# Root of the feed-forward norm: from columns on GpSimd to a row on VectorE, and four PSUM banks more for the first blocks

## The chip, the cores and the metric

The kernel runs on one core of a Trainium2 chip. The metric is device time in microseconds (us), from one launch to its end; lower is better. Five engines work beside each other: TensorE (PE in the profile, with its weight loads as PEld), VectorE (DVE), ScalarE (ACT), GpSimd (POOL) and SyncE (SP), which issues the transfers.

## The reference

One inference step of a two-layer decoder trunk runs over 256 prompt tokens and 8 x 8 sample tokens, 320 in all, with 1024 features. Layer 0 mixes tokens by a gated spatial MLP, layer 1 by an mLSTM. After either comes a feed-forward layer, and ahead of each of the four a norm. What the change touches is the norm ahead of the feed-forward layer and its first blocks:

```python
def rmsnorm(x, g):
    x32 = x.astype(jnp.float32)
    y = x32 * lax.rsqrt(jnp.mean(x32 * x32, axis=-1, keepdims=True) + EPS)
    return (y * g.astype(jnp.float32)).astype(x.dtype)

def conv_ffn(x, buf, w_up, conv_w, conv_b, w_down):
    up = x @ w_up
    a, g = jnp.split(up, 2, axis=-1)
    a_c, new_buf = causal_dwconv(a, buf, conv_w, conv_b)
    y = (jax.nn.gelu(a_c) * g) @ w_down
    return y, new_buf
...
        h = rmsnorm(x, norm_ffn_g[i])
        y, fb = conv_ffn(h, ffn_buf[i], f_w_up[i], f_conv_w[i], f_conv_b[i], f_w_down[i])
        x = x + y
```

All data is fp32.

## The kernel before

Activations stand features by tokens: `xT` is 8 blocks of 128 features by 320 tokens. A product with a weight matrix is made in blocks of 128 output features. `block` (L196) takes one PSUM bank `pm`, and for each of the 8 blocks of input features issues three matmuls of 320 columns (`rows`, L189). They are three because every fp32 operand is split into two fp32r halves, a high one and a low one (`xh`, `xl`, `wh`, `wl`), and high x high, high x low and low x high are summed. So a block of the up projection is 24 matmuls.

The norm's gain is folded into `xh` and `xl` when a residual is finished (`residual_norm`, L309), and the sums of squares are gathered there in `acc`, features on partitions, tokens along the row. The factor of each token, one over the root, is not known when the projection starts. It is applied when a block's result is read out of PSUM: `conv` and `gate` multiply by `rb`, a tile with the factor of all 320 tokens on every partition. So the first blocks of the projection can run before `rb` exists, but their banks stay taken until then.

`rb` is made in three steps. `norm_cols` (L242) makes six matmuls of two columns (three groups of tokens, each as two passes of fp32) that turn `acc` into columns with tokens on partitions (`pc`), VectorE adds the mean's factor and EPS (`ms`), and GpSimd raises the three columns to the power of -1/2 (`rc`). `norm_row` (L270) splits `rc` into halves, VectorE lays them on the diagonal (`dg`, four instructions), two matmuls with ones spread the diagonal to a row on all partitions (`pb`), and ScalarE copies that to `rb`.

In `ffn` (L356) the blocks come in groups of four: two of the conv branch, two of the gate branch. I call the blocks of the up projection p0, p1, p2 and so on. In the first group the order on PE was p0, `norm_cols`, p1, `norm_row`, p2, p3.

Weights come in pieces of 128 x 1024. SP loads them into `raw` (4 buffers), ScalarE casts the high half to `wh` (L167) and VectorE makes the low half `wl` (L168), 3 buffers each. PE's order is pinned to the order in the code; the other engines' queues are set by a scheduler, and each runs its own queue in order.

There are eight PSUM banks: three in the pool `psm`, from which `block` takes, and five in `psa`, for everything else.

Of the kernel before, what the change touches and what calls it, by code (L numbers as in the profile page):

```python
# [9 lines left out]

F32 = mybir.dt.float32
F32R = mybir.dt.float32r
AF = mybir.ActivationFunctionType
ALU = mybir.AluOpType
MULT, ADD, SUB, MAX = ALU.mult, ALU.add, ALU.subtract, ALU.max

P = 128
EPS = 1e-6
# [3 lines left out]
T = TP + NB * NS  # L22
D = 1024
KD = D // P
# [14 lines left out]
class Net:  # L39
# [23 lines left out]
    def weights(self):  # L63
# [19 lines left out]
        def ffn(l):  # L83
# [8 lines left out]
            if l:  # L92
                add(I["f_dnl"], 0, 4, 4, 4, k0=k0)

        ffn(0)
        add(I["b_wg"], 0, 8)
        for h in range(NH):
# [33 lines left out]
    def prefetch(self, n, m):  # L131
# [15 lines left out]
        while len(self.halved) < min(m, len(self.wq)):  # L147
# [6 lines left out]
            else:  # L154
                wh = self.wsp.tile([P, 8, P], F32R, tag="wh", name="wh")
                wl = self.wsp.tile([P, 8, P], F32R, tag="wl", name="wl")
            if self.wq[i][0] is self.I["b_wg"]:
# [35 lines left out]
            self.mm(ps[:, :T], wh[:, k, :], xl, False, False)  # L193
            self.mm(ps[:, :T], wl[:, k, :], xh, False, last and k == kn - 1)

    def block(self, kt, rhs):  # L196

        ps = self.psm.tile([P, 512], F32, tag="pm", name="pm")
        done = 0
        while done < kt:  # L200
            kn = self.wq[self.used][3]
            self.chunk(ps, lambda k: rhs(done + k), done == 0, done + kn == kt)
            done += kn
        return ps
# [5 lines left out]
    def norm_block(self, m, gcol):  # L210
# [3 lines left out]
        g = self.vec(gcol + m)  # L214
        nc.scalar.activation(self.xh[:, m, :], x, AF.Copy, scale=g)
        nc.vector.scalar_tensor_tensor(self.xl[:, m, :], x, g, self.xh[:, m, :].bitcast(F32), op0=MULT, op1=SUB)

    def square_block(self, m):
        nc = self.nc
        x = self.xT[:, m, :]  # L220
        if m == 0:
            self.acc = self.tp.tile([P, T], F32, tag="acc", name="acc", bufs=2)
            nc.scalar.activation(self.acc, x, AF.Square)
        else:
            self.sq = self.tp.tile([P, T], F32, tag="sq", name="sq", bufs=2)
            nc.scalar.activation(self.sq, x, AF.Square)
            nc.vector.tensor_tensor(self.acc, self.acc, self.sq, op=ADD)
# [42 lines left out]
    def norm_row(self):  # L270

        nc = self.nc
        rc = self.tp.tile([P, 2, 3], F32R, tag="rc2h", name="rc_hl", bufs=1)
        self.split(rc[:, 0, :], rc[:, 1, :], self.rc)
        dg = self.tp.tile([P, 2, T], F32R, tag="dg", name="dg", bufs=1)
        rc = rc.bitcast(F32)
        for half in range(2):
            nc.vector.tensor_tensor(
                dg[:, half, :TP].rearrange("p (t c) -> p t c", c=P), self.ident.unsqueeze(1).to_broadcast([P, 2, P]),
                rc[:, half, :2].unsqueeze(2).to_broadcast([P, 2, P]), op=MULT)  # L280
            nc.vector.tensor_scalar(dg[:, half, TP:], self.ident[:, 64:], rc[:, half, 2:3], None, op0=MULT)
        pb = self.psa.tile([P, 512], F32, tag="pa", name="pb")
        for half in range(2):
            self.mm(pb[:, :T], self.ones.bitcast(F32R), dg[:, half, :], half == 0, half == 1)
        rb = self.tp.tile([P, T], F32, tag="rb", name="rb", bufs=1)
        nc.scalar.copy(rb, pb[:, :T])
        self.rb = rb

    def bring(self, m):

        nc, I = self.nc, self.I
        if m == 0:
            nc.sync.dma_start(self.xv[:, :16 + T], I["x0"])
        else:
            nc.sync.dma_start(self.xT[:, m, :], I["xr"][m - 1])
# [31 lines left out]
    def layer_a(self):  # L327
        nc, tc, I, O = self.nc, self.tc, self.I, self.O
        with tc.tile_pool(name="ya", bufs=1) as yp, tc.tile_pool(name="la", bufs=1) as lp:
            yh = yp.tile([P, KA, T], F32R, name="yh_a")  # L330
            yl = yp.tile([P, KA, T], F32R, name="yl_a")
# [65 lines left out]
            def v_gelu(q, pv):  # L397
# [5 lines left out]
                for t in range(2):  # L403
                    nc.scalar.activation(v[:, t, cs], pv[t], AF.Gelu_apprx_tanh, scale=self.rc[:, t:t + 1])
                    nc.vector.bn_stats(st[:, t, q, :], v[:, t, cs])
                nc.scalar.activation(v[r, 2, cs], vs, AF.Gelu_apprx_tanh, scale=self.rc[r, 2:3])
                nc.vector.bn_stats(st[r, 2, q, :], v[r, 2, cs])
# [41 lines left out]
            def normalise(q):  # L449
                for t in range(3):  # L450
                    r = slice(64 if t == 2 else 0, P)
                    vv = v[r, t, q * 512:(q + 1) * 512]
                    nc.scalar.activation(vv, vv, AF.Identity, scale=rs[r, t:t + 1], bias=ve[r, t:t + 1])

# [56 lines left out]
    def ffn(self, l, gnext):  # L511
        nc, tc, I, O = self.nc, self.tc, self.I, self.O
        NPAD = 2 + TP + 10 * NB
        NC = NPAD - 2
        with tc.tile_pool(name=f"yf{l}", bufs=1) as yp, tc.tile_pool(name=f"lf{l}", bufs=1) as lp:
            ext = 0 if gnext is not None else 64
            yh = yp.tile([P, KF, T + ext], F32R, name=f"yh_f{l}")
            yl = yp.tile([P, KF, T], F32R, name=f"yl_f{l}")
            stt = lp.tile([P, KF, 16], F32, name=f"fst{l}")
            nst = lp.tile([P, KF, 18], F32, name=f"fns{l}")  # L520
            nc.sync.dma_start(stt, I["f_state"][l])
            pads = []
            for i in range(3):
                pd = lp.tile([P, NPAD], F32, name=f"fpad{l}_{i}")
                nc.gpsimd.memset(pd[:, 0:2], 0.0)
                pads.append(pd)
            gls = {}

            def conv(b, ps):
                pd = pads[b % 3]  # L530
                ps_ = pd[:, 258:].rearrange("p (b e) -> p b e", e=10)
                nc.gpsimd.tensor_copy(ps_[:, :, 0:2], stt[:, b, :].rearrange("p (b e) -> p b e", e=2))
                nc.vector.tensor_tensor(pd[:, 2:258], ps[:, :TP], self.rb[:, :TP], op=MULT)
                nc.vector.tensor_tensor(ps_[:, :, 2:10], ps[:, TP:T].rearrange("p (b e) -> p b e", e=8),
                                        self.rb[:, TP:].rearrange("p (b e) -> p b e", e=8), op=MULT)
                nc.gpsimd.tensor_copy(nst[:, b, 0:16].rearrange("p (b e) -> p b e", e=2), ps_[:, :, 8:10])
                nc.gpsimd.tensor_copy(nst[:, b, 16:18], pd[:, 256:258])
                cv = lp.tile([P, NC], F32, tag="cv", name="fcv", bufs=3)
                w = V_FW + 66 * l + b
                nc.scalar.activation(cv, pd[:, 0:NC], AF.Identity, scale=self.vec(w), bias=self.vec(V_FB + KF * l + b))  # L540
                for i in (1, 2):
                    nc.vector.scalar_tensor_tensor(cv, pd[:, i:i + NC], self.vec(w + i * KF), cv, op0=MULT, op1=ADD)  # L542
                gl = lp.tile([P, T], F32, tag="gl", name="fgl", bufs=4)
                nc.scalar.activation(gl[:, :TP], cv[:, :TP], AF.Gelu_apprx_tanh)
                nc.scalar.activation(gl[:, TP:].rearrange("p (b e) -> p b e", e=8),
                                     cv[:, 256:].rearrange("p (b e) -> p b e", e=10)[:, :, 2:10], AF.Gelu_apprx_tanh)
                gls[b] = gl

            def gate(b, ps):
                gl = gls.pop(b)  # L550
                y = self.tp.tile([P, T], F32, tag="yf", name="y_f", bufs=2)
                nc.vector.tensor_tensor(y, ps[:, :T], self.rb, op=MULT)
                nc.vector.tensor_tensor(y, y, gl, op=MULT)
                self.split(yh[:, b, :T], yl[:, b, :], y)
                if ext:
                    nc.gpsimd.tensor_copy(yh[:, b, T:], yl[:, b, TP:])

            for i in range(KF // 2):
                b = 2 * i
                p0 = self.block(KD, self.x_rhs)  # L560
                if i == 0:
                    self.norm_cols()
                    p1 = self.block(KD, self.x_rhs)
                    self.norm_row()
                    conv(b, p0)
                    conv(b + 1, p1)
                else:
                    conv(b, p0)
                    conv(b + 1, self.block(KD, self.x_rhs))
                gate(b, self.block(KD, self.x_rhs))  # L570
                gate(b + 1, self.block(KD, self.x_rhs))
            nc.sync.dma_start(O["f_state"][l], nst)
            rhs = lambda k: (yh[:, k, :T], yl[:, k, :])
            if gnext is not None:
                for m in range(KD):
                    self.residual_norm(m, self.block(KF, rhs), gnext)
            else:
                self.final(lambda m: self.block(KF, rhs), yh, yl, lp)
# [792 lines left out]
```

## Time and profile before

| | |
|---|---|
| median of 3 runs | 949.35 us (949.16 to 949.36) |
| the profiled execution | 949.44 us |
| its span, first to last instruction | 947.7 us |
| granted TensorE clock, mean | 0.999 |
| PE busy | 940.8 us (99%) |
| VectorE busy | 675.1 us (71%) |
| ScalarE busy | 517.7 us (55%) |
| GpSimd busy | 85.1 us (9%) |

Layer 0's feed-forward starts at 189.5 us of the span, layer 1's at 704.0 us. In the timeline a row has the start in us, the duration in us, the engine, the line, the operation and the tiles, out of what it reads; a bracket at its end is the idle time ahead of it and what ended that. Matmuls overlap: a row of 0.31 us is followed by the next one's start 0.147 us later, so the cost of a matmul in a stream is the distance of starts, not its duration.

### The profile page before, as it was taken

Reading aid. Unit: us, or ns where it says so; the run is one execution under the profiler, and the core shown is the slowest. Engines: PE = TensorE matmul, PEld = TensorE weight load, DVE = VectorE, ACT = ScalarE, POOL = GpSimd, SP = SyncE. Lnnn points to the kernel's source line nnn. Section 1 sums busy time; section 2 is a strip of 40 time slices with the busy share of each in tenths; the row PEclk is TensorE's granted clock in tenths of the full one; section 3 lists DMA queues with packets and bytes.
Section 4 is the critical chain, followed back from the end, with each engine's and each line's share of the span. In section 5 each row is a group of like instructions: output and inputs, shape, how many; then the busy total and the mean of one; then the engine's idle time right before and its main releaser. Section 6 shows DMA issues by size and latency. Waiting matters only on the chain.

```text
span 947.7 us, 17236 instructions
## 1 busy us (share of the span) xinstructions
PE 940.8 (99%) x6549; PEld 919.5 (97%) x6549; DVE 675.1 (71%) x1244; ACT 517.7 (55%) x940; POOL 85.1 (9%) x300
## 2 busy tenths in 40 slices
PE   9999999999999999999999999999999999999997
PEld 8789999999999999999999999999999999999997
DVE  6668985577777764458898987787778777775542
ACT  7557444354554444347787776575756455444332
POOL 2100000010000000003211001010011111100001
PEclk9999999999999999999999999999999999999999
DMA  8736344444444445456667555734474444445621
GB/s 288 222 126 180 128 141 144 148 153 143 149 156 151 144 148 157 147 169 224 227 204 230 191 187 198 250 124 145 161 213 145 145 157 155 139 147 153 200 85 57
DMA packets 58311, 156.97 MB, mean 166 GB/s; under 512 B 6916, under 2 KB 19852, under 8 KB 58228
## 3 DMA queue, kind: packets, MB, share of 16 engines
q1 hardware_dynamic: 58084, 155.61, 51.2%
q8 instruction: 52, 0.85, 0.4%
q14 instruction: 31, 0.25, 0.1%
q10 hardware_dynamic: 144, 0.26, 0.1%
HBM read 143.89 MB, written 11.95 MB: 164 GB/s over the span
## 4 chain that ended last, share of the span: by engine, by line
PE 99%; ACT 0%; POOLq 0%; DVE 0%; issue 0%; DVEq 0%; ACTq 0%
PE pm L48 83%; PE pv L48 5%; PE num L48 2%; PE pvs L48 2%; PE pyt L48 1%; PE pmix L48 1%; PE py L48 1%; PE psc L48 1%; PE pCp L48 1%; PE pcs L48 1%; PE pv L51 1%; PE phn L51 0%; PE pw L48 0%; PE pk L51 0%; PE pg L48 0%; PE pc L48 0%
## 5 line engine op out<-in xcount | busy, mean ns | idle before, releaser
L167 ACT CAST wh<-raw 128x1024 fp32r<-128x1024 f32 (+4 forms) x252 | 254.5, 1012 | 287.1 <-PE pm L48 154.2
L168 DVE TENSOR_TENSOR wl<-raw,wh 128x1024 fp32r<-128x1024 f32 (+4 forms) x252 | 296.0, 1178 | 117.2 <-ACT wh L167 114.4
L48 PE MATMUL pm<-xh,wh 128*128 128x320 f32 x1216 | 377.9, 311 | 0.0
L48 PE MATMUL pm<-xh,wl 128*128 128x320 f32 x1216 | 375.8, 309 | 0.0
L48 PE MATMUL pm<-xl,wh 128*128 128x320 f32 x1216 | 375.7, 309 | 0.0
L48 PEld LDWEIGHTS pm<-xh,wh 128*128 128x128 f32 x1216 | 228.3, 188 | 0.7
L48 PEld LDWEIGHTS pm<-xl,wh 128*128 128x128 f32 x1216 | 228.4, 188 | 0.0
L48 PEld LDWEIGHTS pm<-xh,wl 128*128 128x128 f32 x1216 | 228.3, 188 | 0.0
L48 PE MATMUL pm<-yh_f,wh 128*128 128x320 f32 x308 | 95.3, 309 | 0.0
L48 PE MATMUL pm<-yh_f,wl 128*128 128x320 f32 x308 | 95.0, 308 | 0.0
L48 PE MATMUL pm<-yl_f,wh 128*128 128x320 f32 x308 | 95.0, 308 | 0.0
L48 PEld LDWEIGHTS pm<-yl_f,wh 128*128 128x128 f32 x308 | 57.8, 188 | 0.0
L48 PEld LDWEIGHTS pm<-yh_f,wh 128*128 128x128 f32 x308 | 57.8, 188 | 0.0
L48 PEld LDWEIGHTS pm<-yh_f,wl 128*128 128x128 f32 x308 | 57.8, 188 | 0.0
L542 DVE SCALAR_TENSOR_TENSOR fcv<-fpad,vecs,fcv 128x336 f32<-128x336 f32 x88 | 49.5, 565 | 2.0 <-ACT fcv L540 0.6
L307 DVE TENSOR_TENSOR xT<-pm,xT 128x320 f32<-128x320 f32 x38 | 18.5, 490 | 31.4 <-PE pm L48 31.4
L48 PE MATMUL pm<-yhb,wh 128*128 128x320 f32 x128 | 40.3, 315 | 0.0
L48 PE MATMUL pm<-yh_a,wh 128*128 128x320 f32 x128 | 39.6, 309 | 0.0
L48 PE MATMUL pm<-yl_a,wh 128*128 128x320 f32 x128 | 39.5, 309 | 0.0
L48 PE MATMUL pm<-yh_a,wl 128*128 128x320 f32 x128 | 39.5, 309 | 0.0
L48 PE MATMUL pm<-yhb,wl 128*128 128x320 f32 x128 | 39.5, 309 | 0.0
L48 PE MATMUL pm<-ylb,wh 128*128 128x320 f32 x128 | 39.5, 309 | 0.0
(321 smaller groups left out, 1350.9 us busy)
## 6 DMA issues: line engine op xcount, KB each, us to landing
raw<-in_f_up SPq DMA_DIRECT2D x88, 512.0 KB, 3.5
raw<-in_b_win SPq DMA_DIRECT2D x48, 512.0 KB, 4.4
raw<-in_f_dn SPq DMA_DIRECT2D x28, 448.0 KB, 3.3
C<-in_C SPq DMA_DIRECT2D x32, 258.0 KB, 5.0
raw<-in_a_win SPq DMA_DIRECT2D x16, 512.0 KB, 3.5
raw<-in_a_wo SPq DMA_DIRECT2D x16, 512.0 KB, 3.6
out_Cs<-C SPq DMA_DIRECT2D x32, 256.0 KB, 3.8
raw<-in_f_dn SPq DMA_DIRECT2D x14, 512.0 KB, 3.5
```

Source lines behind the costliest of these rows:

```text
L48: self.pin(self.nc.tensor.matmul(out, lhsT, rhs, start=start, stop=stop))
L51: self.pin(self.nc.tensor.transpose(out, in_, ident))
L167: self.last_split = nc.scalar.copy(wh[:, c, :], raw[:, c, :])
L168: self.last_low = nc.vector.tensor_tensor(wl[:, c, :], raw[:, c, :], wh[:, c, :].bitcast(F32), op=SUB)
L307: self.nc.vector.tensor_tensor(x, ps[:, :T], x, op=ADD)
L542: nc.vector.scalar_tensor_tensor(cv, pd[:, i:i + NC], self.vec(w + i * KF), cv, op0=MULT, op1=ADD)
```

## The change

Both feed-forward layers lose `norm_cols` and `norm_row`; the two mixers keep them. In their place:

- `norm_spread` splits `acc` itself into two halves, `acc_h` on ScalarE and `acc_l` on VectorE.
- `norm_root` multiplies ones by these halves in two matmuls of 320 columns. The result `pb` holds every token's sum of squares on all partitions. VectorE then takes the root of the whole row: it makes `half` (minus half of the mean with EPS), a first guess from the bits as an integer, and three Newton steps of three instructions, and leaves the result in `rb`. These are 11 instructions on 128 x 320.
- The two matmuls stand inside p1, behind its first two of eight input blocks.
- The blocks p3 to p6 take their banks from `psa` and not from `psm`.

```diff
+I32 = mybir.dt.int32
...
-    def block(self, kt, rhs):
+    def block(self, kt, rhs, ps=None):
 
-        ps = self.psm.tile([P, 512], F32, tag="pm", name="pm")
+        if ps is None:
+            ps = self.psm.tile([P, 512], F32, tag="pm", name="pm")
...
+    def norm_spread(self):
+
+        nc = self.nc
+        ah = self.tp.tile([P, T], F32R, tag="yf", name="acc_h", bufs=2)
+        al = self.tp.tile([P, T], F32R, tag="yf", name="acc_l", bufs=2)
+        self.split(ah, al, self.acc)
+        return ah, al
+
+    def norm_root(self, ah, al):
+
+        nc = self.nc
+        pb = self.psa.tile([P, 512], F32, tag="pa", name="pb")
+        for i, a in enumerate((ah, al)):
+            self.mm(pb[:, :T], self.ones.bitcast(F32R), a, i == 0, i == 1)
+        half = self.tp.tile([P, T], F32, tag="acc", name="half", bufs=2)
+        y = self.tp.tile([P, T], F32, tag="rb", name="rb", bufs=1)
+        s = self.tp.tile([P, T], F32, tag="sq", name="root", bufs=2)
+        nc.vector.tensor_scalar(half, pb[:, :T], -0.5 / D, -0.5 * EPS, op0=MULT, op1=ADD)
+        nc.vector.tensor_scalar(y.bitcast(I32), half.bitcast(I32), -0.5, float(0x5f3759df - 2 ** 30 - 2 ** 22), op0=MULT, op1=ADD)
+        for _ in range(3):
+            nc.vector.tensor_tensor(s, y, half, op=MULT)
+            nc.vector.tensor_tensor(s, s, y, op=MULT)
+            nc.vector.scalar_tensor_tensor(y, s, 1.5, y, op0=ADD, op1=MULT)
+        self.rb = y
...
+            def blk(i, j):
+                return self.block(KD, self.x_rhs, self.psa.tile([P, 512], F32, tag="pa", name="pm")
+                                  if 3 <= 4 * i + j < 7 else None)
+
             for i in range(KF // 2):
                 b = 2 * i
-                p0 = self.block(KD, self.x_rhs)
                 if i == 0:
-                    self.norm_cols()
-                    p1 = self.block(KD, self.x_rhs)
-                    self.norm_row()
-                    conv(b, p0)
-                    conv(b + 1, p1)
-                else:
-                    conv(b, p0)
-                    conv(b + 1, self.block(KD, self.x_rhs))
-                gate(b, self.block(KD, self.x_rhs))
-                gate(b + 1, self.block(KD, self.x_rhs))
+                    parts = self.norm_spread()
+                p0 = blk(i, 0)
+                if i == 0:
+                    p1 = self.psm.tile([P, 512], F32, tag="pm", name="pm")
+                    (wh, wl), _ = self.take()
+                    self.rows(p1, wh, wl, 2, self.x_rhs, True, False)
+                    self.norm_root(*parts)
+                    self.rows(p1, wh[:, 2:, :], wl[:, 2:, :], KD - 2, lambda k: self.x_rhs(2 + k), False, True)
+                conv(b, p0)
+                conv(b + 1, blk(i, 1) if i else p1)
+                gate(b, blk(i, 2))
+                gate(b + 1, blk(i, 3))
```

How the queues stand now is shown at two places of layer 0's feed-forward; layer 1's read alike.

The first place is PE's queue where p0 ends and p1 starts. Before: `pm_2011` is p0's bank, `pm_2050` is p1's, `pc` are the columns.

```order
L48 MATMUL pm_2011<-xh_77,wh_1958 128x320
L48 MATMUL pm_2011<-xl_78,wh_1958 128x320
L48 MATMUL pm_2011<-xh_77,wl_1959 128x320
L48 MATMUL pc_2042<-ones_81,acc_1493 128x2 x3
L48 MATMUL pm_2050<-xh_77,wh_2014 128x320
L48 MATMUL pm_2050<-xl_78,wh_2014 128x320
L48 MATMUL pm_2050<-xh_77,wl_2015 128x320
```

The columns stood between the two blocks, and the two matmuls of the diagonal behind p1.

The same queue now, from p1's second input block on (`pm_2046` is p1's bank; its first input block stands just ahead with three rows of the same form, and p0's last row right ahead of those).

```order
L49 MATMUL pm_2046<-xh_77,wh_2018 128x320
L49 MATMUL pm_2046<-xl_78,wh_2018 128x320
L49 MATMUL pm_2046<-xh_77,wl_2019 128x320
L49 MATMUL pb_2059<-acc_h_2011,ones_81 128x320
L49 MATMUL pb_2059<-acc_l_2012,ones_81 128x320
```

Nothing stands between p0 and p1 any more, and two matmuls of 320 columns stand between p1's sixth and seventh matmul; nothing stands between p1 and p2.

The second place is VectorE's queue from the last addition to `acc` on. Before: `ms`, `rc_hl` and `dg` are the norm's tiles, `wl` is a weight half (that of p3).

```order
L216 SCALAR_TENSOR_TENSOR xl<-xT,vecs,xh 128x320
L227 TENSOR_TENSOR acc<-acc,sq 128x320
L253 TENSOR_SCALAR ms<-pc 128x3
L168 TENSOR_TENSOR wl<-raw,wh 128x1024
L316 TENSOR_TENSOR rc_hl<-rc,rc_hl 128x3
L278 TENSOR_TENSOR dg<-ident,rc_hl 128x256
L281 TENSOR_SCALAR dg<-ident,rc_hl 128x64
```

The last two rows came once more, for the other half, then the weight half of p4 and the first `conv`.

The same queue now (`half`, `root` and `rb` are the tiles of the root):

```order
L218 SCALAR_TENSOR_TENSOR xl<-xT,vecs,xh 128x320
L229 TENSOR_TENSOR acc<-acc,sq 128x320
L343 TENSOR_TENSOR acc_l<-acc,acc_h 128x320
L169 TENSOR_TENSOR wl<-raw,wh 128x1024
L308 TENSOR_SCALAR half<-pb 128x320
L309 TENSOR_SCALAR rb<-half 128x320
L311 TENSOR_TENSOR root<-rb,half 128x320
L312 TENSOR_TENSOR root<-root,rb 128x320
L313 SCALAR_TENSOR_TENSOR rb<-root,rb 128x320
```

`acc_l` stands ahead of p3's weight half. Behind the last row one more `root` row follows, then p4's weight half, the five rows that are left of the three Newton steps, p5's weight half, and only then the two `conv` reads of p0 and p1. On ScalarE the cast `acc_h` stands right behind the last square and ahead of p3's weight cast, and the cast `rc_hl` and the copy `rb` are gone. GpSimd's queue loses the power. SP's queue is the same row for row.

## The prediction

> **What bounds the kernel now.** I read the page's first table and the chain that ended last, then the chain cut to the two places of the change.
>
> ```profile
> PE 940.8 (99%) x6549; PEld 919.5 (97%) x6549; DVE 675.1 (71%) x1244; ACT 517.7 (55%) x940; POOL 85.1 (9%) x300
> PE 99%; ACT 0%; POOLq 0%; DVE 0%; issue 0%; DVEq 0%; ACTq 0%
> 197.65 225.28 PE pm L48 x1536
> 712.59 167.21 PE pm L48 x1140
> ```
>
> PE is the bound from end to end. The last two rows are pieces of the chain: behind the norm of either feed-forward layer PE runs 1536 and 1140 matmuls without a gap, 225.28 / 1536 = 0.1467 us each. That is one slot of 320 columns. So only two things move the time: slots that are added to or taken from PE's queue, and stalls of that queue. Work on the other engines counts only where PE waits for it.
>
> The timeline of PE at layer 0's place:
>
> ```profile
> 192.85 0.31 PE L48 MATMUL pm<-xh,wl 128*128 128x320 f32 x1
> 192.99 0.73 PE L48 MATMUL pc<-ones,acc 128*128 128x2 f32 x6
> 193.58 0.40 PE L48 MATMUL pm<-xh,wh 128*128 128x320 f32 x1
> 193.81 0.32 PE L48 MATMUL pm<-xl,wh 128*128 128x320 f32 x1
> ...
> 197.20 0.46 PE L48 MATMUL pb<-dg,ones 128*128 128x320 f32 x2
> 197.49 0.31 PE L48 MATMUL pm<-xh,wh 128*128 128x320 f32 x1
> ```
>
> And at layer 1's, with the weight loads of `pb` below it:
>
> ```profile
> 707.49 0.72 PE L48 MATMUL pc<-ones,acc 128*128 128x2 f32 x6
> 708.07 0.39 PE L48 MATMUL pm<-xh,wh 128*128 128x320 f32 x1
> ...
> 711.53 0.31 PE L48 MATMUL pm<-xh,wl 128*128 128x320 f32 x1
> 711.77 0.82 PE L48 MATMUL pb<-dg,ones 128*128 128x320 f32 x2
> 712.43 0.31 PE L48 MATMUL pm<-xh,wh 128*128 128x320 f32 x1
> 712.18 0.19 PEld L48 LDWEIGHTS pb<-dg,ones 128*128 128x128 f32 x1 [0.25 <-DVE dg L281]
> ```
>
> In layer 0 the six column matmuls hold p1 back from 192.99 to 193.58, and p1's first matmul takes 0.23 instead of 0.15. The two of the diagonal cost two plain slots. In layer 1 the diagonal also waits: from 711.53 the next slot would be 711.68, and p2 starts at 712.43, 0.75 later instead of 0.29.
>
> **The change on PE: what goes.** From the first column matmul to p2's first one it is 197.49 - 192.99 = 4.50 in layer 0 and 712.43 - 707.49 = 4.94 in layer 1. The new queue has there 24 matmuls of p1 and 2 of the root, all of 320 columns: 26 x 0.1467 = 3.81. If none of them waits, layer 0 gains 0.69 and layer 1 1.13, together 1.82 us. The pair inside a block is taken at two plain slots, as in layer 0 before, where it stood between two blocks; no row of this trace has it inside one.
>
> [...]
>
> **Do the two new matmuls wait?** Their inputs are made after the last addition to `acc`. Rows of VectorE and ScalarE, in that order, the last two a cast of the same size and a handover from ScalarE to VectorE:
>
> ```profile
> 192.26 0.48 DVE L227 TENSOR_TENSOR acc<-acc,sq 128x320 f32<-128x320 f32 x1
> 706.70 0.49 DVE L227 TENSOR_TENSOR acc<-acc,sq 128x320 f32<-128x320 f32 x1
> 190.99 0.46 ACT L226 ACTIVATE sq<-xT 128x320 f32<-128x320 f32 x1
> 193.09 1.05 ACT L167 CAST wh<-raw 128x1024 fp32r<-128x1024 f32 x1 [1.64 <-issue]
> 219.86 0.46 ACT L315 CAST yh_f<-y_f 128x320 fp32r<-128x320 f32 x1
> 223.31 1.23 DVE L168 TENSOR_TENSOR wl<-raw,wh 128x1024 fp32r<-128x1024 f32 x1 [0.43 <-ACT wh L167]
> 222.23 1.05 ACT L167 CAST wh<-raw 128x1024 fp32r<-128x1024 f32 x1 [1.91 <-PE pm L48]
> ```
>
> `acc` is done at 192.74. ScalarE is idle from 191.45, and `acc_h` stands ahead of the cast of 193.09. A handover costs 0.03 (the cast that ends at 223.28, the weight half that starts at 223.31) to 0.05 (the `dg` that ends at 712.13, read at 712.18). So `acc_h` runs 192.78 to 193.24, `acc_l` 193.27 to 193.75, and PE may read it at 193.80. Its slot is 192.99 + 7 x 0.147 = 194.02: 0.22 to spare. In layer 1 `acc` ends at 707.19, 0.45 later that is 707.67 and then 708.25, against a slot at 708.51: 0.26 to spare. Unseen here is only whether both engines hand over that fast at this place. The bounds are nothing and, if `acc_l` came only behind p3's weight half (194.17 + 1.22, then 0.48), 195.92 - 194.02 = 1.9 us per layer. VectorE's queue has it ahead of that half, so I take nothing.
>
> **VectorE's root.** The nearest rows: a read of PSUM, a product of two tiles, a scalar_tensor_tensor, and two pairs in which the second waits for the first.
>
> ```profile
> L552 DVE TENSOR_TENSOR y_f<-pm,rb 128x320 f32<-128x320 f32 x22 | 10.7, 487 | 9.2 <-PE pm L48 9.2
> L542 DVE SCALAR_TENSOR_TENSOR fcv<-fpad,vecs,fcv 128x336 f32<-128x336 f32 x44 | 24.8, 565 | 1.0 <-ACT fcv L540 0.3
> 215.34 0.48 DVE L552 TENSOR_TENSOR y_f<-pm,rb 128x320 f32<-128x320 f32 x1
> 215.85 0.49 DVE L553 TENSOR_TENSOR y_f<-y_f,fgl 128x320 f32<-128x320 f32 x1
> 210.38 1.16 DVE L542 SCALAR_TENSOR_TENSOR fcv<-fpad,vecs,fcv 128x336 f32<-128x336 f32 x2
> L281 DVE TENSOR_SCALAR dg<-ident,rc_hl x8: 241/248/1286, 32.8 to 711.9; 128x64 fp32r<-128x64 f32 x8
> ```
>
> A dependent product follows 0.51 after the one before it, a scalar_tensor_tensor 0.58: 8 x 0.51 + 3 x 0.58 = 5.8 us for the 11 instructions, 0.53 each. The integer one is like no row. I bound each of the 11 by 0.25 below and 1.29 above (the last row's middle and longest) and take 0.53, the rows nearest in size.
>
> In layer 0 p3's weight half ends at 195.4, and `pb` was ready by then. Six of the 11 (3.2), p4's half (1.2), five (2.6) and p5's half (1.2) end at 203.6; then p0 is read, where the trace before has its first read at 199.52.
>
> ```profile
> 199.52 0.42 DVE L533 TENSOR_TENSOR fpad<-pm,rb 128x256 f32<-128x256 f32 x1
> ```
>
> Two covers hide those 4 us. The first is PSUM: on the new clock p1 ends and p2 starts at 192.99 + 3.81 = 196.80, p3 at 200.32, p4 at 203.84, p5 at 207.36, p6 at 210.88 and p7 at 214.40. With three banks p3 would have stood some 4 us; with four more, p7 is the first block that needs one back, ten us after it is free. The second cover is the weights. A block needs its low half at its third matmul. p5's is done at 203.6 and needed at 207.66. p6's has behind p5's half four `conv` reads (1.3), two gate reads and three scalar_tensor_tensor (2.7) and itself (1.2): 208.8, needed at 211.17, 2.4 us to spare. p6 is the tightest. The raw loads wait for these halves and leave up to 1.2 us later; that of p10 is not cast before p7 ends at 217.9. GpSimd and SP are waited for by nobody here. I cost VectorE's part at nothing.
>
> [...]
>
> **The sum.** 949.44 - 1.82 = 947.62 us, with the 1.74 us outside the span unchanged. From the median it is 949.35 - 1.82 = 947.53. About 0.2% (1.9 us) is what a measurement of this kernel can tell from no change, which from the median is 947.45. The forecast lies just short of it.
>
> **The rivals.**
> - The new pair waits for `acc_l`. For it: 0.2 us is little to spare. Against: ScalarE and VectorE are idle there and the queues put both halves first. Late by up to half a microsecond per layer it gives 947.7 to 948.6.
> - The 0.59 us from 192.99 to 193.58 belongs to the restart of a stream and not to the columns, and the new pair inside p1 pays it again. For it: p1's first matmul behind the columns is longer by 0.08. Against: the diagonal's pair had plain slots. Then layer 0 gains 0.69 - 0.59 = 0.10 and layer 1 1.13 - 0.59 = 0.54: 949.44 - 0.64 = 948.8. [...]
> - Slower: the root holds p6's weight half until PE stands. It begins when an operation costs over 0.53 + 2.4 / 11 = 0.75 us, and from 0.83 on (0.91 per layer more) the gain is gone. At the longest row, 1.29, it is 11 x 0.76 - 2.4 = 6.0 per layer, 949.44 - 1.8 + 12.0 = 959.6. For it: 11 instructions in a chain and an integer form that the trace lacks. Against: every row of this size is under 0.6.
>
> **How the numbers follow.** The forecast has 82 in 100, the waiting pair 9, the restart 4, the slow root 5. The time is the forecast's, 947.6. The range goes from 947.2 (runs of the same kernel lie 0.2 apart, and the rounding of the rows) to 948.8, which takes in the first two rivals. Of the forecast's 82 I give 40 to faster by over 0.2%, since the bound lies within 0.1 to 0.2 of it, and 42 to within; the first two rivals are within, and of the slow root 3 are slower and 2 within: 0.40, 0.57, 0.03. For what I have not thought of I move 0.03 from within to slower: 0.40, 0.54, 0.06.
>
> **What would show it.** Right: no `pc` behind either p0; p1 and the pair in 26 starts of 0.147; p2 3.81 after p0's last slot; eleven VectorE rows of about 0.5; the first `fpad` near 203 and no gap on PE up to p8. Wrong: a weight load of `pb` that waits for `acc_l`, or of p5 to p7 that waits for `wl`; a first `pm` behind `pb` longer than 0.31.

## The result, and the profile after

The kernel after the change takes 947.98 us (median of 18 runs, 947.40 to 948.93). Beside it the kernel before takes 949.37 (18 runs, 948.91 to 950.54). The ratio is 0.9983, with an interval of 0.9977 to 0.9989; as a difference that is a gain of 1.04 to 2.18 us. The medians lie 1.39 apart and the two profiled executions 1.91 (949.44 and 947.53), on either side of the forecast 1.82. The gain stands clear of zero, with a middle slightly under the 0.2% that the prediction named as what a measurement can tell.

The page of the kernel after, first its busy times and the chain's shares, then pieces of the chain at the two layers (start, length, line and count):

```profile
PE 938.9 (99%) x6537; PEld 917.8 (97%) x6537; DVE 682.5 (72%) x1256; ACT 517.2 (55%) x938; POOL 89.5 (9%) x298
PE 99%; ACT 0%; POOLq 0%; DVE 0%; issue 0%; DVEq 0%; ACTq 0%
194.22 227.92 PE pm L49 x1554
708.04 169.84 PE pm L49 x1158
```

PE has 12 instructions fewer and is busy 1.9 us less. VectorE has 12 more and is busy 7.4 us more, and nothing of that is in the chain. A slot is still 227.92 / 1554 = 0.1467 us.

The timeline of PE: layer 0 from p0's last slot to p2's first, then layer 1 from p1's first slot to p2's.

```profile
192.74 0.31 PE L49 MATMUL pm<-xh,wl 128*128 128x320 f32 x1
192.88 0.31 PE L49 MATMUL pm<-xh,wh 128*128 128x320 f32 x1
...
193.62 0.31 PE L49 MATMUL pm<-xh,wl 128*128 128x320 f32 x1
193.77 0.31 PE L49 MATMUL pb<-acc_h,ones 128*128 128x320 f32 x1
193.91 0.31 PE L49 MATMUL pb<-acc_l,ones 128*128 128x320 f32 x1
194.06 0.31 PE L49 MATMUL pm<-xh,wh 128*128 128x320 f32 x1
...
196.70 0.31 PE L49 MATMUL pm<-xh,wh 128*128 128x320 f32 x1
706.70 0.31 PE L49 MATMUL pm<-xh,wh 128*128 128x320 f32 x1
...
707.59 0.31 PE L49 MATMUL pb<-acc_h,ones 128*128 128x320 f32 x1
707.73 0.31 PE L49 MATMUL pb<-acc_l,ones 128*128 128x320 f32 x1
...
710.51 0.31 PE L49 MATMUL pm<-xh,wh 128*128 128x320 f32 x1
```

p1 follows p0 after one slot, the pair takes two plain slots, and p2 starts 196.70 - 192.88 = 3.82 after p1 in layer 0 and 710.51 - 706.70 = 3.81 in layer 1, where the kernel before took 4.50 and 4.94. From p1's place in layer 0 to p2's in layer 1 the trace of before has 712.43 - 192.99 = 519.44 us and this one 710.51 - 192.88 = 517.63: 1.81 less. The other 0.1 of the 1.91 is an earlier start of layer 0 (192.88 against 192.99), ahead of p1 and of all that was changed on PE.

### The profile page after: what moved, and what is told of

It is laid out like the page before. It is cut to its first block, busy times and chain, and to the rows that moved or that the text cites. A ratio compares the mean times of both kernels' runs of the same rounds, so it can differ in the third digit from the quotient of the medians.

```text
span 945.7 us, 17201 instructions
## 1 busy us (share of the span) xinstructions
PE 938.9 (99%) x6537; PEld 917.8 (97%) x6537; DVE 682.5 (72%) x1256; ACT 517.2 (55%) x938; POOL 89.5 (9%) x298
## 4 chain that ended last, share of the span: by engine, by line
PE 99%; ACT 0%; POOLq 0%; DVE 0%; issue 0%; DVEq 0%; ACTq 0%
PE pm L49 83%; PE pv L49 5%; PE num L49 2%; PE pvs L49 2%; PE pyt L49 1%; PE pmix L49 1%; PE py L49 1%; PE psc L49 1%; PE pCp L49 1%; PE pcs L49 1%; PE pv L52 1%; PE phn L52 0%; PE pw L49 0%; PE pk L52 0%; PE pg L49 0%; PE pyt L52 0%
```

## The experiments

All are compared with the 947.98 of the kernel after, and each ratio is to the kernel before in runs beside it (medians of 949.31 to 949.49).

### Does PE gain from the columns and the diagonal, or from something else?

**The banks alone.** The kernel before, with its old norm, and the blocks 3 to 6 from the other pool.

```
-                p0 = self.block(KD, self.x_rhs)
+                p0 = blk(i, 0)
...
-                gate(b, self.block(KD, self.x_rhs))
-                gate(b + 1, self.block(KD, self.x_rhs))
+                gate(b, blk(i, 2))
+                gate(b + 1, blk(i, 3))
```

> The kernel before with the changed one's four more banks for p3 to p6 and nothing else; the norm goes by columns and diagonal as before. Slots theory: PE had no gap behind the norm, so the banks bring nothing: the time of before, 949.4, within 0.3. Rival (part of the gain comes from the banks): 0.3 to 1.4 us faster than before. In the trace p2's first matmul comes 4.50 us behind the first column matmul in layer 0 and 4.94 in layer 1, as before.

It takes 949.25 us (ratio 0.9999, 0.999 to 1.0007). In its trace p2's first matmul comes 4.49 and 4.94 us behind the first column matmul. By themselves the banks bring nothing.

**The columns put back.** The kernel after, with six column matmuls between p0 and p1 whose result nobody reads.

```
+                    pc = self.psa.tile([P, 512], F32, tag="pa", name="pc")
+                    for t in range(3):
+                        self.mm(pc[:P, 2 * t:2 * t + 2], self.tokens(self.acc, t), self.ones[:, :2], True, True)
```

> The changed kernel with the six column matmuls put back between p0 and p1; nobody reads their result. Slots theory: they cost what they did, 0.69 us per layer: 1.4 us slower than the changed kernel, 949.3 to 949.4, while the gain of 0.44 on the diagonal's wait in layer 1 stays. Rival (the gain is the restart behind the columns, or the wait for the diagonal alone): 0 to 0.5 us slower than the changed kernel. In the trace: 0.59 from the first column matmul to p1's first, and p1's first matmul longer by 0.08.

It takes 949.38 us (0.9998, 0.9989 to 1.0008): no gain over the kernel before is left that these runs could tell. Its timeline of PE at layer 0:

```profile
193.39 0.72 PE L49 MATMUL pc<-ones,acc 128*128 128x2 f32 x6
193.98 0.39 PE L49 MATMUL pm<-xh,wh 128*128 128x320 f32 x1
194.21 0.31 PE L49 MATMUL pm<-xl,wh 128*128 128x320 f32 x1
```

0.59 for the six and 0.23 for the first slot behind them instead of 0.15: 0.67 us per layer, as in the kernel before. Twice 0.67 is 1.34, and the medians lie 1.40 apart. From p1's place in layer 0 (193.39) to p2's in layer 1 (712.37) the trace has 518.98 us, 1.35 more than the kernel after and 0.46 less than the kernel before. So the diagonal's wait stays gone in the trace; the interval, some 0.9 us to either side, is too wide to show it in the time.

**The columns on narrow weights.** The same over 32 tokens of each part, so that a weight load has 32 columns in place of 128.

```
-                        self.mm(pc[:P, 2 * t:2 * t + 2], self.tokens(self.acc, t), self.ones[:, :2], True, True)
+                        self.mm(pc[:32, 2 * t:2 * t + 2], self.tokens(self.acc, t)[:, :32], self.ones[:, :2], True, True)
```

> The changed kernel with column matmuls between p0 and p1 again, but each over 32 of the 128 tokens only, so that its weight load has 32 columns for 128; nobody reads the result. Loads theory (the columns cost their six weight loads, 0.11 us each): the loads shrink to a quarter, 0.03 us each; from the first column matmul to p1's first 0.15 to 0.25 us, and 0.2 to 0.35 us per layer over the changed kernel: 948.4 to 948.7. Rival (the restart of the stream and the change of the operands' type cost the 0.59): as with the full columns, 0.69 per layer, 949.4.

It takes 948.69 us (0.9991, 0.9982 to 0.9999). Its timeline of PE and of the weight loads, layer 0:

```profile
192.51 0.31 PE L49 MATMUL pm<-xh,wl 128*128 128x320 f32 x1
192.75 0.35 PE L49 MATMUL pc<-ones,acc 128*32 128x2 f32 x6
192.75 0.26 PEld L49 LDWEIGHTS pc<-ones,acc 128*32 128x32 f32 x6 [0.19 <-PE pm L49]
193.03 0.42 PE L49 MATMUL pm<-xh,wh 128*128 128x320 f32 x1
193.28 0.31 PE L49 MATMUL pm<-xl,wh 128*128 128x320 f32 x1
```

The median lies inside the expectation, the trace per layer does not. From p0's last slot at 192.51 to p1's second slot at 193.28 it is 0.77, where two slots take 0.29: 0.48 per layer, not 0.2 to 0.35. So the hit of the median is luck. The six themselves are 0.28 instead of 0.59, so the columns cost less when they are narrower. The load was narrowed and, with it, the matmul's output from 128 partitions to 32; that the load is what counts is argued, and no run separates the two.

The other 0.19 stand outside the six: 0.09 ahead of them, where the first narrow load waits for the matmul ahead of it, and 0.10 in p1's first slot (0.25). With the full columns only the second kind is seen: the six start in their slot, and p1's first slot is 0.08 longer. So breaking the stream cost 0.08 and 0.19 us in these two kernels, and why the narrow load waits is open.

### Has the pair room for its inputs?

The pair's `acc` halves are loaded as weights, and in the kernel after that load starts one slot ahead of the matmul: by 0.14 us in either layer (193.77 against 193.91, 707.59 against 707.73). By then they have to be there: with the pair ahead of p1, below, the two loads wait 0.39 and 0.34 us for them. VectorE's subtraction and the weight load at both layers:

```profile
193.16 0.49 DVE L343 TENSOR_TENSOR acc_l<-acc,acc_h 128x320 fp32r<-128x320 f32 x1 [0.53 <-ACT acc_h L342]
193.77 0.19 PEld L49 LDWEIGHTS pb<-acc_l,ones 128*128 128x128 f32 x1
706.93 0.49 DVE L343 TENSOR_TENSOR acc_l<-acc,acc_h 128x320 fp32r<-128x320 f32 x1 [0.52 <-ACT acc_h L342]
707.59 0.19 PEld L49 LDWEIGHTS pb<-acc_l,ones 128*128 128x128 f32 x1
```

`acc_l` ends at 193.65 and is loaded at 193.77: 0.12 to spare, and 0.17 in layer 1. Two kernels move the pair.

**Ahead of p1:**

```
-                    self.rows(p1, wh, wl, 2, self.x_rhs, True, False)
...
-                    self.rows(p1, wh[:, 2:, :], wl[:, 2:, :], KD - 2, lambda k: self.x_rhs(2 + k), False, True)
+                    self.rows(p1, wh, wl, KD, self.x_rhs, True, True)
```

> The changed kernel with the two matmuls of the norm ahead of p1 and not behind its second input block. Slots theory: they must wait for acc_l. In the changed kernel's trace p1's first slot is 192.88 and acc_l ends at 193.65, read at 193.70: the second of the pair starts at 193.70 where its slot would be 193.03, 0.67 us late in layer 0 and about as much in layer 1: 947.98 + 1.3 = 949.3, all but the time before. The root ends some 0.2 us earlier and nobody gains from it. Rival (two matmuls inside a block cost more than between two blocks): the same time as the changed kernel or less.

It takes 949.44 us (1.0002, 0.9993 to 1.001). Its weight loads in layer 0, with the idle time ahead in brackets:

```profile
193.50 0.19 PEld L49 LDWEIGHTS pb<-acc_h,ones 128*128 128x128 f32 x1 [0.39 <-ACT acc_h L342]
194.03 0.19 PEld L49 LDWEIGHTS pb<-acc_l,ones 128*128 128x128 f32 x1 [0.34 <-DVE acc_l L343]
```

Both loads wait, and p2 is 0.78 us late in layer 0 and 0.76 in layer 1. Without the two input blocks ahead of the pair the gain is gone. The expectation had 0.67. It counted to the start of the second matmul; that matmul does start with its load at 194.03, but the next one follows 0.25 later instead of 0.15. Here the load came only with its matmul, and it cost these 0.10. The long first slot behind the columns has the same mark: in the kernel before p1's first weight load starts at 193.55 and its matmul at 193.58.

**Behind p1's seventh input block** (2 becomes 7 in both calls of `rows`):

> The changed kernel with the two matmuls of the norm behind p1's seventh input block and not behind its second, 15 slots or 2.2 us later. Slots theory: same slots, no wait at either place; the root starts up to 1 us later, since p3's weight half held it until 195.26 anyway, and its covers have 3.6 us: the changed kernel's time, within 0.3. Rival (an earlier row of roots is what brings the gain): 0.5 to 2 us slower than the changed kernel.

It takes 947.74 us (0.9983, 0.9974 to 0.9992), the same as the kernel after within the noise, and PE has no gap there. More room brings nothing, since the pair did not wait.

### What covers VectorE's root?

**Three banks.** The first blocks from the one pool again:

```
-                return self.block(KD, self.x_rhs, self.psa.tile([P, 512], F32, tag="pa", name="pm")
-                                  if 3 <= 4 * i + j < 7 else None)
+                return self.block(KD, self.x_rhs)
```

> The changed kernel, but p3 to p6 take their banks from psm again, so that three banks must do. Slots theory (the gain is PE's slots alone, and the root's 8 us on VectorE are hidden by the four more banks): p3 waits on PE until p0's bank is read. That read ends at 203.45 of the changed kernel's span and p3 starts there at 200.22, so PE stands 3.2 us in either layer: 947.98 + 6.5 = 954.5, slower than before. Rival (the banks are not needed, the reads come early enough or the weights hide it): no change from 947.98. In the trace: one gap on PE of 3.2 us at p3 in either layer, none at p4.

It takes 957.83 us (1.0086, 1.0072 to 1.0099), 9.85 more than the kernel after. Its timeline of PE at p3, and the windows around it (busy time and count of PE, PEld, DVE, ACT and POOL, then the granted clock, the share of the DMA engines and GB/s), with p0's last read on VectorE as the first row:

```profile
203.11 0.21 DVE L561 TENSOR_TENSOR fpad<-pm,rb 128x64 f32<-128x64 f32 x1
199.95 0.31 PE L49 MATMUL pm<-xh,wl 128*128 128x320 f32 x1
203.47 0.61 PE L49 MATMUL pm<-xh,wh 128*128 128x320 f32 x1 [3.22 <-DVE fpad L561]
203.88 0.47 PE L49 MATMUL pm<-xl,wh 128*128 128x320 f32 x1
204.15 0.47 PE L49 MATMUL pm<-xh,wl 128*128 128x320 f32 x1
```

```profile
200.00:203.40 3.40, 0.26 (x2) 0.00 (x0) 3.30 (x8) 1.04 (x1) 0.14 (x2) 0.93 0.51 154
203.40:206.40 3.00, 2.93 (x11) 2.96 (x12) 2.85 (x8) 1.86 (x5) 0.98 (x6) 0.52 0.60 180
206.40:210.00 3.60, 3.60 (x27) 3.60 (x26) 1.83 (x4) 1.96 (x5) 0.14 (x1) 1.00 0.00 0
```

p3 stands 3.52 - 0.15 = 3.4 us, where 3.2 was expected, until p0 has been read (at 203.32), and so in layer 1 (3.47 between two starts). What was not expected is what follows. For about 3 us the granted clock is 0.52 and slots come 0.27 apart (204.15 - 203.88), then it is 1.00. The eleven slots from 203.47 on take 2.98 us where 1.61 is plain, 1.37 more, and in layer 1 it is 1.46. With the two stops, 3.37 + 3.32 + 1.37 + 1.46 = 9.5 stands against 9.5 us more of span (955.2 against 945.7).

The slots 0.27 apart come here behind 3.22 us of idle time by the bracket, and in layer 1 behind 3.17. With six Newton steps, below, a granted clock of 0.56 comes behind 2.49.

**One bank** of the other pool, for p3 alone (`if 4 * i + j == 3`):

> The changed kernel with one bank more for three: p3 takes its bank from psa, p4 and all later ones from psm as before. Slots theory: the first bank that is needed back is then p0's, for p4. In the changed kernel's trace p4 starts at 203.74 and p0 has been read at 203.45, 0.24 us earlier with the handover; p5 needs p1's bank 3.4 us after it is free. So there is no wait and the time is the changed kernel's, 947.7 to 948.2: one of the four banks does the work. Rival (the four banks are needed because everything behind the root runs 4 us late): a wait of 1 to 4 us at p4 or p5 in either layer, 950 to 956, and with a wait of over 2.5 us the half clock that the kernel with three banks showed.

It takes 947.75 us (0.9983, 0.9975 to 0.9992), with no gap on PE in either feed-forward layer. In its timeline, p0's last read on VectorE and the first matmul of p4, which takes p0's bank here:

```profile
203.84 0.21 DVE L561 TENSOR_TENSOR fpad<-pm,rb 128x64 f32<-128x64 f32 x1
204.35 0.31 PE L49 MATMUL pm<-xh,wh 128*128 128x320 f32 x1
```

The bank is free at 204.05 and taken in its slot at 204.35. So one bank more is just enough for a root of this length; the other three are room that it doesn't need.

**A longer root.** More Newton steps, three VectorE instructions each, beyond the three that it has: the count in `for _ in range(3)` becomes 5, 6 and 9.

> The changed kernel with five Newton steps for three, 3.1 us more on VectorE per layer. Six steps had held p7's weight half until PE stood 2.8 and 2.0 us, and my count for it had looked at p6's half alone. Counted through VectorE's queue for p7 and p8 this time: p7's half is done near 212.7 and needed at 214.5, p8's near 217.5 and needed at 218.1. Covers theory: no stall, or up to 0.5 us at p8, and no half clock: 948.0 to 949.0. Rival (any longer root costs its length): 3.1 us per layer, 954.2.

> The changed kernel with six Newton steps for three: nine more instructions of 0.52 us, 4.7 us per layer, on VectorE. Slots theory with its covers: in the changed kernel's trace the tightest weight half (p6) is done 3.6 us ahead of its use and the banks have 11 us to spare; the scheduler now puts p6's half ahead of the conv reads. So PE stands 0 to 1.1 us per layer: 948.0 to 950.2, and I take 948.0 to 948.5. Rival (the root sits on the path that sets the end): 4.7 us per layer, 957.4.

> The changed kernel with nine Newton steps for three: eighteen more instructions, 9.4 us per layer on VectorE. Slots theory with its covers: the root now ends 9.4 us later, which is more than the weights have to spare (3.6 to 4.6 us in the changed kernel's trace) and less than the banks have (11 us). PE stands 2 to 6 us per layer, waiting for weight halves (wl) of p6 to p9: 952 to 960. If the scheduler takes all halves ahead of the root's steps, only the banks bind and it is near 948. Rival (the root sits on the path): 9.4 us per layer, 966.8.

| steps | instructions of the root | us | ratio to before | PE stands (between two starts), layer 0; layer 1 |
|---|---|---|---|---|
| 3 | 11 | 947.98 | 0.9983 (0.9977 to 0.9989) | nowhere |
| 5 | 17 | 948.38 | 0.999 (0.9981 to 0.9999) | 0.25 (one long slot); 0.43 |
| 6 | 20 | 954.50 | 1.0048 (1.0035 to 1.0061) | 2.80; 2.01 |
| 9 | 29 | 958.76 | 1.01 (1.0086 to 1.0114) | 1.94 and 4.22; 1.95, 1.20 and 0.37 |

The waits of PE with six steps, and below them with nine (us in total, times, the longest):

```profile
PE pm L49 <- DVE wl L169: 4.2, 2, 2.5
```

```profile
PE pm L49 <- DVE wl L169: 4.8, 2, 3.9
PE pm L49 <- DVE fpad L561: 3.3, 2, 1.6
```

With five steps p8's weight half is just late in both layers, as the expectation allowed. In layer 0 the load comes only with its matmul:

```profile
218.28 0.19 PEld L49 LDWEIGHTS pm<-xh,wl 128*128 128x128 f32 x1
218.29 0.41 PE L49 MATMUL pm<-xh,wl 128*128 128x320 f32 x1
218.54 0.31 PE L49 MATMUL pm<-xh,wh 128*128 128x320 f32 x1
```

PE doesn't stand, but the slot is 0.25: 0.10 lost. In layer 1 the stop is 0.43 and the slot behind it 0.25 as well: 0.38. Together it is 0.48 us; the medians lie 0.40 apart, which is no more than noise could make. With six the expectation, 948.0 to 948.5, was wrong by 6 us. Its timeline of PE and VectorE in layer 0, then windows of it behind the stops in either layer:

```profile
214.72 0.31 PE L49 MATMUL pm<-xl,wh 128*128 128x320 f32 x1
216.26 1.21 DVE L169 TENSOR_TENSOR wl<-raw,wh 128x1024 fp32r<-128x1024 f32 x1
217.52 0.42 PE L49 MATMUL pm<-xh,wl 128*128 128x320 f32 x1 [2.49 <-DVE wl L169]
```

```profile
217.50:221.40 3.90, 3.88 (x16) 3.88 (x17) 3.90 (x7) 0.91 (x3) 0.36 (x2) 0.56 0.41 134
738.40:742.00 3.60, 3.55 (x24) 3.55 (x25) 3.60 (x6) 0.63 (x2) 0.24 (x1) 1.00 0.67 157
```

It isn't p6's weight half that comes late, the only one that the expectation looked at, but p7's. The longer root pushes the reads of p0 to p5 and the work behind them together, the queue has seven microseconds of this ahead of p7's half, and it starts at 216.26 when PE wants it at 214.87. In layer 1 it is p8's. PE stands 2.65 and 1.86 us, and behind the first stop the granted clock is 0.56 for 3.9 us, some 1.6 us more. The clock falls only behind the restart: the slot from 217.78 to 217.93 is still plain. In layer 1 two long slots, one behind the stop and one at p7's half, add 0.10 each. That is 6.3 us, where the medians lie 6.5 apart and the spans of the two profiles 6.7.

Nine steps lie inside the expectation of 952 to 960, in part by luck. It had the banks 11 us to spare, and p7 waits for p0's bank in both layers: with three more weight halves ahead of p0's reads, p7 starts in layer 0 at 216.39, after 1.63 us of idle time that the last of them ended. In layer 0 p9's half makes the stop of 4.22 us, with a granted clock of 0.52 behind it, which the expectation did not price.

## Why the prediction was right

The forecast was 947.6 us, in a range of 947.2 to 948.8. 947.98 lies inside, 0.4 above the middle.

- **PE bounds the kernel, so only slots and stalls count.** Held. VectorE got 7.4 us more to do and the time fell. What the new queue gains is its count of slots and the wait that is gone, not the banks and not an earlier root.
- **Columns and diagonal go, 0.69 and 1.13 us.** Held in the trace to 0.02: 4.50 became 3.82 and 4.94 became 3.81. The columns put back cost 1.34 of it. The rest is the diagonal's pair, whose two slots in layer 0 are matched by the new pair's, and whose wait of 0.44 in layer 1 has gone; that wait is read from traces, and no run takes it away alone. By the median of 18 runs the gain is 1.39, by the profiled executions 1.91, and the interval holds both. Two kernels with the same slots, the pair behind the seventh input block and the one bank, lie 1.75 and 1.58 below the kernel before in the runs beside them. So the 1.82 is well within what was measured, and all three medians lie somewhat under it.
- **The pair takes two plain slots and waits for nothing.** Held, with less room than given. The prediction measured 0.22 and 0.26 us to the matmul's slot; what reads the halves is the load, 0.14 us earlier, and it leaves 0.12 and 0.17. The pair ahead of p1 shows the price when the room is gone, 0.76 to 0.78 per layer. That is more than the 0.5 of the rival, since there the pair stands six slots earlier.
- **The columns' 0.59 us is theirs and not the restart's.** Held: at a pair of 320-column slots inside p1 no restart is paid, the full columns start in their slot, and narrower columns take 0.28 for 0.59. The 0.08 of p1's first slot does belong to the restart; the prediction saw it and had it in its sum of 0.69. The 0.11 us for each load that the expectation for the narrow columns started from was its author's estimate. In the kernel before, the six loads start at 192.86 and the next one at 193.55, 0.69 / 6 = 0.115 each. With 32 columns it is 192.75 to 193.03, 0.28 / 6 = 0.047 each, where the expectation had 0.03: the quarter was not shown, and 0.28 is more than its 0.15 to 0.25.
- **Root of 5.8 us, hidden.** It was shorter. VectorE's timeline of the kernel after in layer 0:

```profile
195.26 0.48 DVE L308 TENSOR_SCALAR half<-pb 128x320 f32<-128x320 f32 x1
195.78 0.33 DVE L309 TENSOR_SCALAR rb<-half 128x320 int32<-128x320 int32 x1
196.13 0.49 DVE L311 TENSOR_TENSOR root<-rb,half 128x320 f32<-128x320 f32 x1
...
201.35 0.49 DVE L313 SCALAR_TENSOR_TENSOR rb<-root,rb 128x320 f32<-128x320 f32 x1
...
202.90 0.42 DVE L560 TENSOR_TENSOR fpad<-pm,rb 128x256 f32<-128x256 f32 x1
...
206.24 1.22 DVE L169 TENSOR_TENSOR wl<-raw,wh 128x1024 fp32r<-128x1024 f32 x1
```

  From 195.26 to 201.84 it is 6.58, with p4's weight half (1.14 from start to start) inside: 5.4 us. The scalar_tensor_tensor at 320 columns takes 0.49, not the 0.57 of 336, and the integer step 0.33. p0 is read at 202.90 instead of 203.6, and p6's half ends at 207.46, not 208.8: 3.6 us to spare instead of 2.4. Dependent operations of the Newton steps start 0.52 to 0.53 apart, where the prediction's rows had 0.51 and 0.58.
- **The banks are the first cover.** Held: without them the time is 957.83. The stall of some 4 us that the prediction named was 3.4, and the half clock behind it, 1.4 to 1.5 us per layer, was missing from the price. One of the four banks would have done.
- **A slow root turns it.** Held in direction, and the point was close. Five steps, 3.1 us more root by 6 x 0.52, give the first stops; the prediction had them begin at p6 after 2.4 us more. But the blocks that stop are p7 and later, because the scheduler orders the queue anew. Taken as a straight line from p6 the price was too low: six steps are nine instructions more, 9 x 0.52 = 4.7 us, which less p6's 3.6 would be 1.1 per layer, and 6.5 us are measured for both.

## What to carry to other kernels

When one engine is busy 99% of the time, a rewrite that gives another engine more work can still pay: count the slots that leave the first one, and then find the cover of the work on the second, which here is one PSUM bank and the lead of the weight halves. Work in the matmul's shape, two 320-column slots inside a running block, cost 0.29 us where six 2-column matmuls with six weight loads cost 0.67. The operands that were loaded as weights were due at their load, 0.14 us before the matmul; a load that came only with the matmul cost 0.10 us here. And a wait of PE is to be priced with the clock that follows it: up to 2.0 us no more than a first slot that was 0.1 longer, and from 2.8 us on 1.4 to 1.6 us more in these runs.

## What the hardware showed that was not expected

- **The half clock (granted 0.52 to 0.56) after a stop.** Stops of 1.20, 1.94, 1.95 and 2.01 us (between two starts) left the clock at 1.00 in the windows behind them; after 2.80, 3.47, 3.52 and 4.22 us slots came some 0.267 apart for nine to twelve matmuls, 2.4 to 3.2 us. For the 1.94 and the 4.22 in layer 0 of the nine steps:

```profile
216.40:220.00 3.60, 3.60 (x25) 3.60 (x26) 3.60 (x10) 2.21 (x6) 1.03 (x5) 1.00 0.18 73
227.90:231.10 3.20, 3.20 (x12) 3.20 (x13) 3.20 (x6) 0.67 (x1) 1.74 (x2) 0.52 0.65 175
```

  The shortest stop with the half clock behind it is the 2.80 between two starts, 2.49 of idle time by the bracket above, in the one trace that has it. Between 2.0 and 2.8 no run says anything.
- **The integer step** of VectorE on 128x320 words took 0.33 us, beside 0.48 for the tensor_scalar that reads PSUM and 0.49 for the products.
